# State-space preparation in the bank of the key sums, and five gate tiles tied to products of the last quarter

## The chip, the core and the metric

The kernel runs on one core of one Trainium2 chip. The metric is device time in microseconds (us), as the median of several runs. The core has five engines that run side by side, each working through its own instructions in a fixed order: TensorE (PE in the profile; PEld is its weight load), VectorE (DVE), ScalarE (ACT), GpSimd (POOL) and SyncE (SP, which here issues nearly all DMAs). TensorE writes its results to PSUM, which the kernel uses as eight banks of 512 fp32 values per partition; DVE and ACT read them from there.

## The reference

One layer of a hybrid decoder, for 512 prompt tokens and 64 sampled tokens (8 sequences of 8), 576 tokens together, width 1024:

```python
def layer(h, p, conv_buf, shift_buf, ssm0, wkv0, w):
    mix, ... = token_mixers(rmsnorm(h, w['norm_mix']), conv_buf, shift_buf, ssm0, wkv0, w)
    h = h + mix
    hf = rmsnorm(h, w['norm_ffn'])
    h = h + (jax.nn.silu(hf @ w['w_gate']) * (hf @ w['w_up'])) @ w['w_down']
    gate = jax.nn.sigmoid(rmsnorm(h, w['norm_ple']) @ w['w_ple_gate'])
    h = h + gate * (p.astype(h.dtype) @ w['w_ple_proj'])
    return h, ...
```

`token_mixers` projects the normalised input once (`w_in`) and splits the columns between two groups. Group A is a state-space mixer: a short convolution over x, B and C, then per head a decayed state in chunks of 128 tokens; its output is multiplied by silu(z), where z is one block of eight 128-channel tiles of the projection, and normalised. Group B is a delta-rule mixer (16 heads, 64 x 64 state per head):

```python
s = (s * w_t[:, :, None, :] - s_kk[..., None] * (kk_t * a_t)[:, :, None, :]
     + v_t[..., None] * k_t[:, :, None, :])
return s, jnp.einsum('bhvk,bhk->bhv', s, r_t)
```

Both outputs, side by side, go through `w_out` and are added to h.

## The kernel before

**Layout.** Channels lie on partitions, the 576 tokens on the free axis. A linear product of one 128-channel output tile (`linear`, `mm3`, lines 213 to 215) splits weights and inputs into a high and a low part in fp32r and runs three matmuls for each 128-row block of the weights and each half of the tokens (288). Weights are loaded in blocks of 512 columns (`raw`, three buffers), then split by ACT (`whi`) and by POOL or DVE in turn (`wlo`, line 198), two buffers each.

**Group B.** The heads are taken in four quarters. For each: `prep` (keys, decays), `start_states`, `gram` (small products), `solve` (a triangular inverse, column by column on DVE, lines 654 and 656), `combine` (the two halves of the inverse joined: the products of line 678 and line 692), `chain` (nine windows g of 64 tokens in turn; `core` of a window starts with the products of line 769, then the products of 777, 782, 792, 801) and `head_norm` (the centring products of line 879, token sums, and a norm). `solve` and `combine` of the last quarter are traced after `head_norm` of the third.

**Gate tiles.** The eight z tiles (`zed`: one `linear`, then two ACT passes, one DVE product and a store of `hz` to DRAM) are the last entries of a list of projections. `fill()` takes the next entry. Three z tiles are taken inside `inverse(Q[3])`, between `solve` and `combine`; the other five by the letters "z" of `SEQ = "zzszszszspyw"`, after the last quarter's `chain`. The texts call them z1 to z8.

**State space.** `ssd` is a generator; each "s" of `SEQ` runs it to its next `yield`, and the rest runs after the last head norm. Its preparation: decay rows turned to token order (line 1015), chunk decays (1030), then for five token windows w in the order 1, 2, 3, 4, 0 the B transposes (1044) and the B-C products (1048), and then for each window the x transposes (1065), the scaled x (`xdt`, `xe`) and the state (1078, `hin`). With "p" the per-layer input projection is made, with "y" the finished rows of group B are read back, with "w" one partial output tile. After the generator's end come the output projection (`residual`, line 1265), then `scaled` for the two halves of group A (line 1297).

**PSUM.** Pool `lin` has two tiles of two banks. Pool `sq` has `cx` (two banks), `tr` (one) and `cb` (one). `cb` holds the key sums of `prep` and the start states; it has no other use. When the last head norm is done, `sq` gives way to the pool `ps2`: `r`, `y` (one bank each) and `d` (two).

**Order.** The framework orders each engine's instructions when the program is built: an instruction may run as soon as its inputs, its buffer and its engine are free by the framework's own estimate of durations, and among those that may, the one traced first goes first. The order is then fixed, and semaphores make an engine wait where an input is late. `tc.issue_after(ins)` adds one rule for a block of the program: its instructions on the engine of `ins` are placed behind `ins` in that engine's order. Nothing waits for `ins` to end.

Of the kernel before, what the change touches and what calls it, by code (L numbers as in the profile page):

```python
# [74 lines left out]
def hybrid_step(ctx, tc, A):  # L75
# [20 lines left out]
    def lin_bank():  # L96
        turn[0] += 1
        return lins[turn[0] // 2 % len(lins)].tile([P, 1024], F32, tag="lin", name=nm("lin"))
# [155 lines left out]
    def cb_ps():  # L254
        return bank(sq_, "cb", 1)
# [405 lines left out]
    def combine(s):  # L661

        TT = s.TT = inverses[s.q % 2]
        AA = s2.tile([P, 9, 2, 32], F32, tag="AA", name=nm("AA"))
        for e in range(2):
            for z in range(2):
                r0 = e * 64 + z * 32
                nc.sync.dma_start(TT[r0:r0 + 32, :, :, z * 32:z * 32 + 32].rearrange("s g j t -> s (g j) t"),
                                  s.Td[z, e].rearrange("g s t -> s g t"))
            nc.sync.dma_start(AA[e * 64:e * 64 + 32].rearrange("s g j t -> s (g j) t"),  # L670
                              s.Ad[e].rearrange("g s t -> s g t"))
        Wp = cx_ps()
        Wv = Wp[:].rearrange("p (g j t) -> p g j t", g=8, j=2)
        for g in range(1, 9):
            for jj in jj2:
                for e in range(2):
                    lo_, hi_ = e * 64, e * 64 + 32
                    T.matmul(Wv[hi_:hi_ + 32, g - 1, jj, :], s.Lst[lo_:lo_ + 32, g, jj, 32:64],
                             AA[lo_:lo_ + 32, g, jj, :], start=True, stop=True)
        for e in range(2):  # L680
            hi_ = e * 64 + 32
            if e:
                act(AA[hi_:hi_ + 32, 1:9], Wv[hi_:hi_ + 32], scale=-1.0)
            else:
                V.tensor_scalar(AA[hi_:hi_ + 32, 1:9], Wv[hi_:hi_ + 32], -1.0, None, ALU.mult)
        Xp = cx_ps()
        Xv = Xp[:].rearrange("p (g j t) -> p g j t", g=8, j=2)
        for g in range(1, 9):
            for jj in jj2:
                for e in range(2):  # L690
                    lo_, hi_ = e * 64, e * 64 + 32
                    T.matmul(Xv[lo_:lo_ + 32, g - 1, jj, :], AA[hi_:hi_ + 32, g, jj, :],
                             TT[hi_:hi_ + 32, g, jj, 32:64], start=True, stop=True)
        for e in range(2):
            lo_ = e * 64
            if e:
                act(TT[lo_:lo_ + 32, 1:9, :, 32:64], Xv[lo_:lo_ + 32])
            else:
                V.tensor_copy(TT[lo_:lo_ + 32, 1:9, :, 32:64], Xv[lo_:lo_ + 32])
# [19 lines left out]
    def chain(s):  # L719
# [45 lines left out]
        def core(g):  # L765
            sv = suv(g)
            xw = pairs(cx_ps())
            for jj in jj2:
                T.matmul(xw[:, jj], flat(Gt[:, g, jj, 0]), sv[:, jj, 0], start=True, stop=True)
            xs = sp.tile([P, 2, 64], F32, tag="xs", name=nm("xs"), bufs=2)  # L770
            act(xs[H[0]], xw[H[0], :, 0])
            V.tensor_copy(xs[H[1]], xw[H[1], :, 1])
            ups = cx_ps()
            uw = ups[:].rearrange("p (j v) -> p j v", j=8)
            for jj in jj2:
                for e in range(2):
                    T.matmul(uw[H[e], jj, :], TT[H[e], g, jj, :], xs[H[e], jj, :], start=True, stop=True)
            outs[g] = ow = singles(cx_ps())
            for jj in jj2:
                for e in range(2):  # L780
                    rho = s.Z[H[e], jj, 1, :] if g == 0 else AR[H[e], jj, g]
                    T.matmul(ow[H[e], jj], sv[H[e], jj, 0, e], rho, start=jj == 0, stop=False,
                             skip_group_check=True)
            act(sv[H[0], :, 1, 0], uw[H[0], 0:2, :], scale=-1.0)
            V.tensor_scalar(sv[H[1], :, 1, 1], uw[H[1], 0:2, :], -1.0, None, ALU.mult)
# [62 lines left out]
            if g == 1:  # L848
                sampled()

    YR = []

    def pair(q, name):
        return (se, sp)[q % 2].tile([P, 2, NT], F32, tag=f"bk{q % 2}", name=nm(name), bufs=2)
# [11 lines left out]
    def head_norm(s, ahead=()):  # L866

        q = s.q
        st = tr_ps()[:, 0:20]
        Oc = []  # L870
        gsq = None if ahead else pair(q, "gsq")
        if not ahead:
            ahead = [gate_bonus(2 * q), gate_bonus(2 * q + 1)]
        for jj in jj2:
            o = s.AR[:, jj].rearrange("p g t -> p (g t)")
            sq = gsq[:, jj] if gsq else sp.tile([P, NT], F32, tag="gt", name=nm("gsq"), bufs=2)
            for a, b in HV:
                pp = cx_ps()
                T.matmul(pp[:, 0:HALF], cen[:], o[:, a:b], start=True, stop=True)
                V.tensor_copy(o[:, a:b], pp[:, 0:HALF])  # L880
                act(sq[:, a:b], pp[:, 0:HALF], AF.Square)
            token_sums(st, jj, sq)
            Oc.append(o)
        rn = inv_norm(st, "gnr", 1.0 / 64, GN_EPS)
        for jj in jj2:
            j = 2 * q + jj
            o = Oc[jj]
            gt, y = ahead[jj]
            for a, b, ps in by_channel(rn, jj, cx_ps, "rxg"):
                V.scalar_tensor_tensor(o[:, a:b], o[:, a:b], par("ln_x_w", j), ps, ALU.mult, ALU.mult)  # L890
            (V if q == 3 else G).tensor_tensor(y, y, o, ALU.add)
            yo = sp.tile([P, NT], F32, tag="gt", name=nm("yo"), bufs=2)[:] if q == 2 and jj else y
            V.scalar_tensor_tensor(yo, y, par("ln_x_b", j), gt, ALU.add, ALU.mult)
            if q < 3:
                nc.sync.dma_start(yr_d[j][:], yo)
            else:
                YR.append(split(y, xp, ("xhi", "xlo"), [P, NT], lo_eng=G))

# [39 lines left out]
    def d_ps():  # L938
        return bank(late[2], "d", 2)
# [32 lines left out]
    def ssd():  # L972
# [34 lines left out]
                        ac[:, 64:NT].rearrange("p (b t) -> p b t", b=4), ALU.subtract)  # L1007
        act(de[:], de[:], AF.Exp)
        tk = mt("tk", [P, 5, 3, 16])
        big = lin_bank()  # L1010
        ps = big[:, 0:512]
        for w, (a, m) in enumerate(SW):
            for i, src in enumerate((dt, ac, de)):
                o = (3 * w + i) * 16
# [8 lines left out]
        def sel(h):  # L1023
# [2 lines left out]
        dr = mt("dr", [16, 12, 16])  # L1026
        V.tensor_tensor(dr[:], ident[0:16, 0:16].unsqueeze(1).to_broadcast([16, 12, 16]),
                        al[:].unsqueeze(2).to_broadcast([16, 12, 16]), ALU.mult)
        ps = big[:, 512:1024]
        T.matmul(ps[:, 0:192], ones[0:16, :], dr[:].rearrange("p a b -> p (a b)"), start=True, stop=True)  # L1030
        DEC = mt("DEC", [P, 12, 16])
        act(DEC[:].rearrange("p a b -> p (a b)"), ps[:, 0:192], AF.Exp)
# [5 lines left out]
        xd, hin = {}, [None]  # L1038
        for w in (1, 2, 3, 4, 0):
            a, m = SW[w]  # L1040
            big = lin_bank()
            ps = big[:, 0:512]
            for g in range(2):
                T.transpose(ps[0:m, g * P:g * P + P], BT[g][:, a:a + m], ident[:])
            act(Bt[0:m, w, :], ps[0:m, 0:256])
            ps = big[:, 512:1024]
            for g in range(2):
                T.matmul(ps[0:m, g * m:g * m + m], BT[g][:, a:a + m], CT[g][:, a:a + m], start=True, stop=True)
            if w:
                V.tensor_tensor(CBm[:, :, w - 1, :], ps[:, 0:256].rearrange("p (g q) -> p g q", g=2),  # L1050
                                cmask[:].unsqueeze(1).to_broadcast([P, 2, P]), ALU.mult)
            else:
                V.tensor_tensor(CBd[:], ps[0:64, 0:128].rearrange("p (g q) -> p g q", g=2),
                                dgmask[0:64, 1, :].unsqueeze(1).to_broadcast([64, 2, 64]), ALU.mult)
        yield
        for w in (1, 2, 3, 4, 0):
            a, m = SW[w]
            xt = xd[w] = k4("xdt", [P, D])
            xe = mt("xe", [P, D], bufs=2)
            big = lin_bank()  # L1060
            for h in range(2):
                ps = big[:, h * 512:h * 512 + 512]
                c = slice(h * 512, h * 512 + 512)
                for i in range(4):
                    T.transpose(ps[0:m, i * P:i * P + P], xs[4 * h + i][:, a:a + m], ident[:])
                V.tensor_tensor(h16(xt[0:m, c]), h16(ps[0:m, :]),
                                tk[0:m, w, 0, h * 8:h * 8 + 8].unsqueeze(2).to_broadcast([m, 8, 64]), ALU.mult)
                G.tensor_tensor(h16(xe[0:m, c]), h16(xt[0:m, c]),
                                tk[0:m, w, 2, h * 8:h * 8 + 8].unsqueeze(2).to_broadcast([m, 8, 64]), ALU.mult)
            if w:  # L1070
                if w == 3:
                    yield
                hn = k4("hin", [P, D])
                big = lin_bank()
                for g in range(2):
                    c = slice(g * 512, g * 512 + 512)
                    ps = big[:, c]
                    T.matmul(ps[:], Bt[:, w, g * P:g * P + P], xe[:, c], start=True, stop=True)  # L1078
                    if w > 1:
                        G.tensor_tensor(h16(hn[:, c]), h16(hin[-1][:, c]),  # L1080
# [149 lines left out]
    next(steps)  # L1230
    chain(Q[3])
    parts = 0
    for what in SEQ:
        if what == "z":
            fill()
        elif what == "s":
            next(steps)
        elif what == "p":
# [286 lines left out]
```

## Time and profile before

| | us |
|---|---|
| median of 3 runs | 1372.16 |
| runs | 1371.36 to 1374.79 |
| the profiled execution | 1371.14 |
| its span in the profile | 1369.4 |
| TensorE busy | 1262.0 |
| DVE busy | 718.5 |
| ACT busy | 575.8 |
| POOL busy | 551.2 |

The span is the time between the first and last instruction of the profiled execution. A busy matmul row counts a matmul from its start to its modelled end, and matmuls overlap, so single rows add up to more than the elapsed time; the busy times of a stretch do not. The granted clock is the share of full speed at which TensorE was allowed to run in a stretch. In timeline rows the first number is the start and the second the duration, in us; a bracket at the end gives the idle time before the instruction and what ended it. Most ACT work shows as line 92, a helper, and all linear products as lines 213 to 215; tile names tell them apart.

### The profile page before, as it was taken

To read this page: it belongs to the slowest core of one execution; us is meant where nothing else is said; L and a number is where in the kernel's file an instruction comes from. 1 tells how busy PE (TensorE), PEld (TensorE's weight loads), DVE (VectorE), ACT (ScalarE), POOL (GpSimd) and SP (SyncE) were. 2 spreads that over 40 slices of the span, in tenths; PEclk is the share of its full clock that TensorE was granted. 3 is DMA by queue.
4 is the path that set the end of the run, shared out by engine and by line. 5 is a ranking of instruction groups with operands and counts; after the bars stand their busy time and mean duration, and the time that the engine had idled before them with its cause. 6 is when DMAs were issued, how large, how long until landed. Compare 5 with 4: busy or idle time off the path is not lost.

```text
span 1369.4 us, 26331 instructions
## 1 busy us (share of the span) xinstructions
PE 1262.0 (92%) x10565; PEld 1162.5 (85%) x10565; DVE 718.5 (52%) x1333; ACT 575.8 (42%) x1148; POOL 551.2 (40%) x543
## 2 busy tenths in 40 slices
PE   6897899999989979889969999999999999999996
PEld 5786897889868858777748889999999999999995
DVE  6648767697778787744276674522222221111265
ACT  6565346534662553334433463333233232222253
POOL 5326415632452253124365656433333333343442
PEclk9998999899979989979969999999999999999998
DMA  4322242234223313432625533222322222223332
GB/s 161 123 70 62 84 119 88 70 100 123 67 78 91 104 56 95 131 131 98 191 88 173 185 104 86 67 80 85 80 83 86 83 80 82 81 78 85 125 115 69
DMA packets 94458, 135.56 MB, mean 99 GB/s; under 512 B 34704, under 2 KB 39056, under 8 KB 94336
## 3 DMA queue, kind: packets, MB, share of 16 engines
q1 hardware_dynamic: 94336, 133.88, 32.2%
q8 instruction: 83, 1.36, 0.4%
q14 instruction: 39, 0.32, 0.1%
HBM read 106.10 MB, written 27.75 MB: 98 GB/s over the span
## 4 chain that ended last, share of the span: by engine, by line
PE 41%; DVE 4%; ACT 3%; POOL 2%; DMA 2%; issue 1%; DVEq 0%; ACTq 0%; POOLq 0%
PE lin L215 12%; PE lin L213 12%; PE lin L214 12%; POOL wlo L198 1%; DMA raw<-wts 1%; PE d L1131 1%; PE y L1181 1%; PE d L1143 1%; DVE pg L1373 1%; ACT whi L92 1%; ACT L92 0%; DVE h L1374 0%; ACT wp L92 0%; PE lin L1078 0%; DVE h L1391 0%
## 5 line engine op out<-in xcount | busy, mean ns | idle before, releaser
L213 PE MATMUL lin<-xhi,whi 128*128 128x288 f32 (+1 forms) x1488 | 451.7, 304 | 4.0 <-ACT whi L92 2.2
L215 PE MATMUL lin<-xhi,wlo 128*128 128x288 f32 (+1 forms) x1488 | 448.7, 302 | 2.9 <-POOL wlo L198 2.9
L214 PE MATMUL lin<-xlo,whi 128*128 128x288 f32 (+1 forms) x1488 | 448.8, 302 | 0.0
L198 POOL TENSOR_TENSOR wlo<-raw,whi 128x512 fp32r<-128x512 f32 x136 | 182.1, 1339 | 478.2 <-ACT whi L92 437.1
L92 ACT ACTIVATE whi<-raw 128x512 fp32r<-128x512 f32 (+1 forms) x272 | 168.8, 621 | 408.5 <-PE lin L214 349.2
L213 PEld LDWEIGHTS lin<-xhi,whi 128*128 128x128 f32 (+1 forms) x1488 | 282.3, 190 | 11.3 <-issue 2.8
L215 PEld LDWEIGHTS lin<-xhi,wlo 128*128 128x128 f32 (+1 forms) x1488 | 283.0, 190 | 9.4 <-POOL wlo L198 3.8
L214 PEld LDWEIGHTS lin<-xlo,whi 128*128 128x128 f32 (+1 forms) x1488 | 282.6, 190 | 4.6 <-issue 1.5
L198 DVE TENSOR_TENSOR wlo<-raw,whi 128x512 fp32r<-128x512 f32 (+1 forms) x136 | 95.5, 702 | 165.4 <-ACT whi L92 163.0
L215 PE MATMUL lin<-ah,wlo 128*128 128x288 f32 x352 | 105.1, 299 | 0.9
L213 PE MATMUL lin<-ah,whi 128*128 128x288 f32 x352 | 104.1, 296 | 0.0
L214 PE MATMUL lin<-al,whi 128*128 128x288 f32 x352 | 103.9, 295 | 0.0
L215 PEld LDWEIGHTS lin<-ah,wlo 128*128 128x128 f32 x352 | 66.3, 188 | 3.3 <-POOL wlo L198 2.6
L214 PEld LDWEIGHTS lin<-al,whi 128*128 128x128 f32 x352 | 66.1, 188 | 0.0
L213 PEld LDWEIGHTS lin<-ah,whi 128*128 128x128 f32 x352 | 66.0, 188 | 0.0
L1332 DVE TENSOR_TENSOR sg<-lin,sg 128x576 f32<-128x576 f32 x22 | 16.7, 758 | 82.9 <-PE lin L215 81.7
L1327 DVE TENSOR_TENSOR sg<-lin,rstd 128x576 f32<-128x576 f32 x22 | 16.7, 758 | 69.3 <-PE lin L215 69.0
L654 DVE TENSOR_TENSOR tmp<-L,Tt 72x30 f32<-72x30 f32 (+14 forms) x120 | 50.2, 418 | 3.2
L213 PE MATMUL lin<-xu,whi 128*128 128x288 f32 x128 | 39.8, 312 | 9.1 <-ACT xu L92 7.5
L656 DVE TENSOR_TENSOR Tt<-Tt,tmp 72x30 f32<-72x30 f32 (+14 forms) x120 | 45.1, 376 | 3.5
L215 PE MATMUL lin<-xu,wlo 128*128 128x288 f32 x128 | 39.9, 313 | 6.5 <-DVE wlo L198 5.4
L186 POOL TENSOR_TENSOR al<-sg,ah 128x576 fp32r<-128x576 f32 x22 | 31.5, 1432 | 32.1 <-ACT ah L92 32.1
(364 smaller groups left out, 2516.5 us busy)
## 6 DMA issues: line engine op xcount, KB each, us to landing
raw<-wts SPq DMA_DIRECT2D x271, 256.0 KB, 2.6
S<-s_wkv SPq DMA_DIRECT2D x8, 512.0 KB, 5.0
hd<-s_ssm SPq DMA_DIRECT2D x8, 512.0 KB, 4.8
o_ssm_s<-hd SPq DMA_DIRECT2D x8, 512.0 KB
xbc_d<-E SPq DMA_DIRECT2D x12, 288.0 KB, 2.1
x<-xT SPq DMA_DIRECT2D x8, 288.0 KB
gate_d<-g SPq DMA_DIRECT2D x8, 288.0 KB, 2.6
bv_d<-rw SPq DMA_DIRECT2D x8, 288.0 KB
```

Of the source, the lines that this page charges most:

```text
L92: S.activation(out, in_, func, bias=bias, scale=scale)
L186: eng.tensor_tensor(lo[:], src, hi[:].bitcast(F32), ALU.subtract)
L198: eng.tensor_tensor(lo[:, 0:n], raw[:, 0:n], hi[:, 0:n].bitcast(F32), ALU.subtract)
L213: T.matmul(ps[:, a:b], whi, xhi[:, a:b], start=first, stop=False)
L214: T.matmul(ps[:, a:b], whi, xlo[:, a:b], start=False, stop=False)
L215: T.matmul(ps[:, a:b], wlo, xhi[:, a:b], start=False, stop=last)
L654: V.tensor_tensor(o, L[:, jx:jx + 1, jx + 1:32].to_broadcast([NB, jx, n]), Tt[:, 0:jx, jx:jx + 1].to_broadcast([NB, jx, n]), ALU.mult)
L656: V.tensor_tensor(Tt[:, 0:jx, jx + 1:32], Tt[:, 0:jx, jx + 1:32], o, ALU.subtract)
L1131: T.matmul(yo[(h % 2) * 64:(h % 2) * 64 + 64, (h // 2) * 8:(h // 2) * 8 + 8], hd[:, h * 64:h * 64 + 64], cd[:, h, b * 8:b * 8 + 8], start= ...
L1143: T.matmul(ps[:], bm[:, i, g * P:g * P + P], xst[:, c], start=i == 0, stop=i == 1)
L1327: V.tensor_tensor(s_[:], ps, rs[:], ALU.mult)
L1332: V.tensor_tensor(s_[:], up, s_[:], ALU.mult)
```

## The change

The state-space preparation's tiles move from `lin` to `cb`, with both halves in one bank; the tiles of the later windows (x transposes of w = 4 and 0, states of w = 3 and 4) move to `d`. The kernel records five kinds of small product in `marks` (the last one traced under a key stays), and each of the five z tiles of `SEQ` is placed behind one of them in TensorE's order: z4 behind the last centring product of the third quarter's head norm, z5 behind the last product of line 678 in the last quarter, z6, z7 and z8 behind the first products of windows 1, 2 and 3 of the last quarter's chain.

```diff
-                    T.matmul(Wv[hi_:hi_ + 32, g - 1, jj, :], s.Lst[lo_:lo_ + 32, g, jj, 32:64],
-                             AA[lo_:lo_ + 32, g, jj, :], start=True, stop=True)
+                    marks["c", s.q] = T.matmul(Wv[hi_:hi_ + 32, g - 1, jj, :], s.Lst[lo_:lo_ + 32, g, jj, 32:64],
+                                               AA[lo_:lo_ + 32, g, jj, :], start=True, stop=True)
...
-                T.matmul(xw[:, jj], flat(Gt[:, g, jj, 0]), sv[:, jj, 0], start=True, stop=True)
+                marks[q, g] = T.matmul(xw[:, jj], flat(Gt[:, g, jj, 0]), sv[:, jj, 0], start=True, stop=True)
...
-    YR = []
+    YR, marks = [], {}
...
-                T.matmul(pp[:, 0:HALF], cen[:], o[:, a:b], start=True, stop=True)
+                marks["n", q] = T.matmul(pp[:, 0:HALF], cen[:], o[:, a:b], start=True, stop=True)
...
         tk = mt("tk", [P, 5, 3, 16])
-        big = lin_bank()
-        ps = big[:, 0:512]
+        big = cb_ps()
+        ps = big[:, 0:256]
...
-        ps = big[:, 512:1024]
+        ps = big[:, 256:512]
         T.matmul(ps[:, 0:192], ones[0:16, :], dr[:].rearrange("p a b -> p (a b)"), start=True, stop=True)
...
             a, m = SW[w]
-            big = lin_bank()
-            ps = big[:, 0:512]
+            big = cb_ps()
+            ps = big[:, 0:256]
...
-            ps = big[:, 512:1024]
+            ps = big[:, 256:512]
...
             xe = mt("xe", [P, D], bufs=2)
-            big = lin_bank()
             for h in range(2):
-                ps = big[:, h * 512:h * 512 + 512]
+                ps = cb_ps() if w in (1, 2, 3) else d_ps()
...
                 hn = k4("hin", [P, D])
-                big = lin_bank()
                 for g in range(2):
                     c = slice(g * 512, g * 512 + 512)
-                    ps = big[:, c]
+                    ps = cb_ps() if w < 3 else d_ps()
...
     parts = 0
+    places = [("n", 2), ("c", 3), (3, 1), (3, 2), (3, 3)]
     for what in SEQ:
         if what == "z":
-            fill()
+            with tc.issue_after(marks[places.pop(0)].ins):
+                fill()
```

## The prediction

> **What bounds the kernel now.** I read the page's head, then busy time and granted clock by stretches, then the timeline of each engine where TensorE is not full. TensorE is busy for 92% of the span, so only places where it idles, or runs at half clock, can give time back.
>
> ```profile
> span 1369.4 us, 26331 instructions
> PE 1262.0 (92%) x10565; PEld 1162.5 (85%) x10565; DVE 718.5 (52%) x1333; ACT 575.8 (42%) x1148; POOL 551.2 (40%) x543
> ```
>
> Stretches: start:end, length, then busy time of PE, PEld, DVE, ACT, POOL with counts, granted clock, DMA share, GB/s.
>
> ```profile
> 528.00:569.00 41.00, 40.83 (x357) 37.60 (x357) 36.06 (x92) 14.05 (x31) 6.96 (x8) 1.00 0.37 125
> 569.00:605.00 36.00, 28.04 (x314) 21.64 (x312) 18.33 (x41) 17.13 (x38) 7.68 (x10) 0.67 0.56 171
> 605.00:673.00 68.00, 62.12 (x551) 51.20 (x549) 25.29 (x61) 26.09 (x64) 23.73 (x21) 1.00 0.36 119
> 673.00:686.00 13.00, 13.00 (x86) 10.17 (x86) 2.94 (x6) 6.67 (x13) 8.43 (x6) 0.76 0.54 157
> 686.00:715.00 29.00, 18.66 (x102) 12.34 (x102) 22.71 (x33) 9.44 (x20) 18.07 (x15) 0.62 0.29 103
> 715.00:808.00 93.00, 91.24 (x830) 80.77 (x831) 57.41 (x106) 44.21 (x104) 54.55 (x46) 0.94 0.51 162
> 808.00:839.00 31.00, 30.57 (x267) 29.80 (x266) 19.63 (x25) 11.73 (x19) 20.85 (x14) 1.00 0.24 70
> 900.00:1000.00 100.00, 100.00 (x752) 100.00 (x751) 21.45 (x31) 30.42 (x47) 30.67 (x24) 1.00 0.29 82
> ```
>
> The last row prices a linear matmul: 100/752 = 0.133 us. A gate tile is 8 x 2 x 3 = 48 of them, 6.4 us. Two holes lie in the stage that is changed. From 569 to 605 (end of the third quarter, start of the last quarter's chain) TensorE holds 28.04 x 0.67 = 18.8 us of full-clock work in 36: 17.2 us free. From 686 to 715 it holds 18.66 x 0.62 = 11.6 in 29: 17.4 us free. After 715 it is full (91.24 of 93, 30.57 of 31), so what is put into the holes comes off the end if the state-space part keeps up.
>
> Why gate tiles do not fill the first hole:
>
> ```profile
> 569.76 0.63 ACT L92 ACTIVATE hz<-lin 128x576 f32<-128x576 f32 x1
> 604.83 0.40 PE L1048 MATMUL lin<-bc,bc 128*64 128x64 f32 x4
> 605.15 0.40 PE L213 MATMUL lin<-xhi,whi 128*128 128x288 f32 x1
> 619.27 1.12 PE L1078 MATMUL lin<-xe,Bt 128*128 128x512 f32 x2 [0.51 <-POOL xe L1068]
> 619.83 0.70 PE L213 MATMUL lin<-xhi,whi 128*128 128x288 f32 x1
> ```
>
> The fifth gate tile (z5) is out at 569.76. z6 starts at 605.15, 0.3 us after the last product of the state-space window loop, z7 right after a product of the next step. Both users take `lin` tiles, and these are handed out in the order of the program: z6 stands behind six state-space tiles.
>
> **The change part by part.** No arithmetic is added or removed; buffers move, and five gate tiles get a place in TensorE's order.
>
> A. *z4 and z5 leave the solve stage.* They ran before 569 and may now issue only behind these products, given by line (count: shortest/median/longest ns, first to last start): z4 behind the last L879, z5 behind the last L678, z6 to z8 behind the first three cores of the chain (L769, four matmuls each).
>
> ```profile
> L879 PE MATMUL cx<-ar,cen x4: 406/458/510, 571.6 to 573.1; 128*128 128x288 f32 x4
> 582.31 1.92 PE L678 MATMUL cx<-AA,Lst 32*32 32x32 f32 x64 [0.44 <-DVE ar L890]
> L769 PE MATMUL cx<-suv,G x12: 272/422/582, 588.1 to 612.9; 128*128 128x128 f32 x12
> ```
>
> That takes 12.8 us of TensorE work out of 528 to 569, where DVE sets the pace (36.06 of 41, the solve's row updates, with no TensorE in them). On DVE each gate tile costs one weight half and one product:
>
> ```profile
> 559.10 0.68 DVE L198 TENSOR_TENSOR wlo<-raw,whi 128x512 fp32r<-128x512 f32 x1
> 564.60 0.75 DVE L391 SCALAR_TENSOR_TENSOR hz<-thz,hz 128x576 f32<-128x576 f32 x1
> ```
>
> Best case 2 x 1.43 = 2.9 us gained. Against it: with little left for TensorE its clock may fall, as it did at 569 to 605 (0.67), and the small products then take twice as long (L769: 272 ns at best, 582 at worst). A chain step has four groups of them, together about 1.6 us; the last one and a half steps would lose 2.4 us. I take -1, nearer to the DVE row, because the small products also stop waiting behind gate matmuls. The Trainium skill ("TensorE: Matmul & The Clock Gate", Part 1) says that TensorE drops to half rate after an idle window of about 3.4 us and needs as long a busy one to return. By that rule, with the rows' 2.4 us as its price, this part is +2.4 and the result 1363 instead of 1360; the clock row of 569 to 605 agrees in that a part-filled stretch ran at 0.67, and no run yet shows it for the solve stage.
>
> B. *569 to 605.* z4 and z5 and, from about 589, z6 can run here: 19.2 us into 17.2 us of free time, so about 2 us spill over. The clock stays up: L879, L678, the second product group of the inverse, the chain's first cores. The products on the path at low clock are L678's 1.92 us, the inverse's second group of the same size, the head norm's L879 (four at 0.46) and two L769 groups (four at up to 0.58 each): about 8 us, of which half comes back: -4. Each of some 20 hand-overs now finds one or two gate matmuls in front (0.13 to 0.3 us): +4. Net +2: the -4 and +4 cancel and the spill stays; bounds -2 and +6. The tiles' other work has cover: each brings two weight loads and a store on SP's queue, four ACT passes of 0.63 (2.5 us), one split of 1.27 on POOL, 1.43 on DVE; the stretch holds ACT 17.13, POOL 7.68 and DVE 18.33 of 36. A Tanh between the root and the exponential can add one table load at most:
>
> ```profile
> 569.93 1.27 POOL L198 TENSOR_TENSOR wlo<-raw,whi 128x512 fp32r<-128x512 f32 x1 [7.79 <-ACT whi L92]
> L92 ACT ACT_TABLE_LOAD x2 | 2.6, 1283 | 0.4 <-DVE smask L1004 0.3
> ```
>
> 1.3 us, and not where a Tanh follows an exponential (none is loaded by z6 at 616), so I take nothing.
>
> C. *605 to 673.* Here TensorE is full (62.12 of 68), and one tile (z6) is gone: at the stretch's density of 0.91 that is 6.4 x 0.91 = -5.8, or nothing where the chain's own hand-overs become the bound. z7 and z8 move up inside the stretch; the per-layer projection and the partial output follow them without waiting for state-space tiles, which changes the order and not the sum. A, B and C: -1 + 2 - 5.8 = about -5.
>
> D. *The state-space preparation in one `cb` bank.* Both halves now share a bank and one buffer, so transposes, copy, products and mask of a window follow each other:
>
> ```profile
> L1044 PE MATMUL lin<-ident,bc x2: 474/474/474, 589.4 to 590.0; 128*128 128x128 f32 x2
> L1048 PE MATMUL lin<-bc,bc x20: 219/276/580, 594.9 to 605.0; 128*128 128x128 f32 x16, 128*64 128x64 f32 x4
> 600.04 0.38 ACT L92 ACTIVATE Bt<-lin 128x256 f32<-128x256 f32 x1
> ```
>
> Two transposes at 0.47, the copy 0.38, four products at 0.28 to 0.58, a mask taken as long as the copy: about 3 us a window, 15 us for five, as long as the loop takes now (589.4 to 605.2). The transposes and states of w=1 to 3, ten more fills of the bank, lose the overlap of copy and products, about 1 us each. What needs them is the part after the last head norm, which starts with the rows of L1108 at 692 (below): 0 on the path, covered by the chain from 605 to 673.
>
> E. *686 to 715.* The last windows (w=3 state, w=4, w=0) leave `lin` for the two `d` banks.
>
> ```profile
> L1108 PE MATMUL d<-r,idr x16: 400/401/421, 692.3 to 695.6; 128*128 128x64 f32 x16
> L1078 PE MATMUL lin<-xe,Bt x6: 801/1061/1062, 702.5 to 710.0; 128*128 128x512 f32 x6
> 695.74 1.40 POOL L186 TENSOR_TENSOR xlo<-gb,xhi 128x576 fp32r<-128x576 f32 x1 [1.41 <-ACT xhi L92]
> 714.75 0.61 PE L213 MATMUL lin<-xhi,whi 128*128 128x288 f32 x1
> ```
>
> The output projection's inputs are complete at 695.74 + 1.40 = 697.1, but its first matmul runs at 714.75: until then both `lin` tiles belong to the state-space part. Freed, it can start at about 698. Of these 17 us some 6 are state-space work at full clock, so up to 11 us of projection moves up. Against it: the decay rows (L1108) stood in `d` at 692, beside the `lin` work; now eight tiles take the two `d` banks ahead of them. At about 1 us of products (L1078) and as much of DVE and hand-over, four rounds are 8 to 11 us by which the sampled part starts later. DVE, which is nearly full there (22.71 of 29), would have held part of that anyway. How far it counts is read at the end of the mixing:
>
> ```profile
> L1265 DVE TENSOR_TENSOR h<-lin,yl x1: 757/757/757, 807.9 to 807.9; 128x576 f32<-128x576 f32 x1
> L317 DVE RECIPROCAL rn<-rn x1: 175/175/175, 822.6 to 822.6; 128x5 f32<-128x5 f32 x1
> L1297 DVE TENSOR_TENSOR yl<-lin,bc x1: 757/757/757, 838.7 to 838.7; 128x576 f32<-128x576 f32 x1
> ```
>
> The rows are the last projection tile (L1265), the second root of the state-space part (L317), and the last of the first eight scaled tiles (L1297). The second half of that part is ready at 822.6 and wanted at 838.7: 16 us of slack. So TensorE's gain passes and the delay mostly vanishes in the slack. Bounds -11 and +5; I take -7.
>
> Sum: -5 - 7 = -12. The profiled execution took 1371.14 us (span 1369.4), 1 us under the median of 1372.16; 1371 - 12 = 1359, against the median 1360.
>
> **Rivals.** *Half:* only the first hole pays. In the second, projection matmuls now stand in TensorE's order between the products of a part that starts up to 11 us later; if both together cost it the 16 us of slack and the 7 of E, E is 0: 1372 - 5 = 1367. For it: eight tiles in two banks, and DVE that can't hurry; against it: TensorE, once it has less projection left, is freer for that part. *Nothing:* the work only changes places, since the solve stage idles by what the first hole gains, and the projection's first tile still waits for something else: about 1371. *Slower:* weights behind the state-space loads.
>
> ```profile
> 590.00:595.00 5.00, 3.00 (x32) 2.55 (x31) 2.86 (x9) 3.54 (x7) 0.00 (x0) 0.50 1.00 356
> ```
>
> Just where z5 and z6 shall run, the DMA engines are full with twelve loads of 288 KB, some 10 us at 356 GB/s. TensorE runs in order; a gate tile whose weights lie behind these loads holds the chain's products behind it. One such stall of 11 us, with A at -1 and E halved (-3.5), is +6.5: 1379. It decides from 8 us of stall. For it: the share of 1.00; against it: three raw and two split buffers are loaded ahead.
>
> **How the numbers follow.** Forecast 0.50, half 0.18, nothing 0.14, slower 0.18. Under 0.3% (4 us) a measurement of this kernel can't be told from no change. Faster 0.50 + 0.14 of the half case (which lies just past that bound) = 0.64, same 0.04 + 0.14 = 0.18, slower 0.18. The likeliest case's own range is 1350 to 1367 (E at -11 with C whole and B at -2, or E at -2). Unknown ends widen it: both holes filled whole (about 1346), and the stalled case up to 1377, with a tenth left out above and a little below.
>
> **What would show it.** Gate matmuls between 570 and 605 at a granted clock near 1.0; the last quarter's chain ending about 5 us earlier; the solve stage no longer than 41 us, TensorE part idle in it; the first output projection matmul within 3 us of the last head norm's split; 715 to 839 still full. The prediction is wrong if the chain's first products wait for L213 to L215 or their weights, if the solve stage grows, or if TensorE idles before the second half of the scaled tiles.

## The result, and the profile after

| | before | after |
|---|---|---|
| median, us | 1371.91 (20 runs) | 1365.46 (20 runs) |
| lowest to highest, us | 1368.42 to 1380.77 | 1359.87 to 1371.88 |
| ratio after / before | | 0.9949, 95% interval 0.9932 to 0.9965 |
| the profiled execution, us | 1371.14 | 1370.43 |

The changed kernel is 6.5 us faster (0.51%); forecast were 12. Its profiled execution was one of its slower ones and says by its own total almost nothing, so it is read stage by stage. The page's head, after:

```profile
span 1368.7 us, 26325 instructions
PE 1259.1 (92%) x10565; PEld 1160.4 (85%) x10565; DVE 719.6 (53%) x1333; ACT 577.4 (42%) x1148; POOL 550.2 (40%) x543
```

Five rows of the timelines cut the section that was changed into a front and a back: the first row product of the last solve (L647), the last split of the last head norm (xlo, L186), and the three roots by token of L317 (first and second half of the state-space part, then the feed-forward norm). After:

```profile
537.54 0.69 DVE L647 TENSOR_SCALAR Tt<-L 72x1024 f32<-72x1024 f32 x1 [3.29 <-DMA L<-Ld]
696.40 1.43 POOL L186 TENSOR_TENSOR xlo<-gb,xhi 128x576 fp32r<-128x576 f32 x1 [1.40 <-ACT xhi L92]
807.70 0.19 DVE L317 RECIPROCAL rn<-rn 128x5 f32<-128x5 f32 x1 [1.19 <-ACT rn L92]
829.55 0.19 DVE L317 RECIPROCAL rn<-rn 128x5 f32<-128x5 f32 x1 [0.73 <-ACT rn L92]
881.48 0.19 DVE L317 RECIPROCAL rn<-rn 128x5 f32<-128x5 f32 x1 [2.61 <-ACT rn L92]
```

Before:

```profile
530.26 0.69 DVE L647 TENSOR_SCALAR Tt<-L 72x1024 f32<-72x1024 f32 x1 [3.12 <-DMA L<-Ld]
802.12 0.19 DVE L317 RECIPROCAL rn<-rn 128x5 f32<-128x5 f32 x1 [3.00 <-ACT rn L92]
822.58 0.17 DVE L317 RECIPROCAL rn<-rn 128x5 f32<-128x5 f32 x1
884.12 0.19 DVE L317 RECIPROCAL rn<-rn 128x5 f32<-128x5 f32 x1 [2.61 <-ACT rn L92]
```

Front, from the solve to the split: 165.5 before (the split stood at 695.74), 158.9 after. Back, from the split to the third root: 188.4 and 185.1. All later times are counted from these marks, since the execution after reached the solve 7.3 us late. A second profile of the unchanged kernel (last experiment) was as late, at 537.41, so that lateness needs no change to explain it.

What TensorE did in between, by stretches cut at each kernel's own events: solve, then up to the chain's first product, the chain, the head norm up to the split, and 0 to 20, 20 to 80 and 80 to 120 us behind the split. Columns as in the prediction. Before:

```profile
530.26:566.74 36.48, 36.31 (x307) 33.52 (x306) 33.85 (x89) 13.22 (x28) 6.96 (x8) 1.00 0.33 111
566.74:588.08 21.34, 15.38 (x221) 11.68 (x221) 12.18 (x24) 9.27 (x20) 5.64 (x8) 0.74 0.58 155
588.08:671.30 83.22, 76.84 (x665) 63.16 (x663) 32.53 (x79) 33.49 (x81) 25.77 (x23) 0.92 0.39 132
671.30:695.74 24.44, 19.25 (x122) 15.51 (x118) 12.21 (x21) 9.41 (x17) 11.22 (x8) 0.73 0.63 197
695.74:715.74 20.00, 13.34 (x75) 7.54 (x74) 14.56 (x21) 8.18 (x18) 16.02 (x14) 0.59 0.08 33
715.74:775.74 60.00, 60.00 (x595) 52.72 (x595) 35.62 (x70) 22.27 (x57) 37.27 (x33) 0.96 0.53 174
775.74:815.74 40.00, 38.24 (x300) 34.96 (x300) 29.49 (x46) 25.13 (x51) 22.13 (x15) 0.91 0.42 130
```

After:

```profile
537.54:574.24 36.70, 32.52 (x274) 27.98 (x273) 33.75 (x94) 11.65 (x27) 5.75 (x7) 0.91 0.28 91
574.24:595.82 21.58, 17.84 (x227) 16.50 (x226) 11.06 (x20) 10.22 (x19) 5.62 (x8) 0.76 0.61 170
595.82:674.41 78.59, 77.03 (x694) 63.44 (x689) 32.03 (x79) 34.70 (x85) 26.09 (x24) 1.00 0.44 148
674.41:696.40 21.99, 17.23 (x107) 11.56 (x103) 12.74 (x21) 8.92 (x17) 11.22 (x8) 0.85 0.64 200
696.40:716.40 20.00, 18.85 (x133) 17.35 (x132) 10.74 (x16) 4.40 (x8) 11.28 (x10) 0.99 0.37 117
716.40:776.40 60.00, 60.00 (x625) 53.88 (x625) 39.09 (x70) 26.78 (x65) 40.20 (x35) 1.00 0.47 161
776.40:816.40 40.00, 31.52 (x252) 26.43 (x251) 31.73 (x51) 24.48 (x53) 25.25 (x19) 0.87 0.41 120
```

Take a stretch's length less its busy time times its clock: the TensorE time lost in it (an estimate, as the clock is a mean over the stretch). The first four stretches lose 0.2 + 10.0 + 12.5 + 10.4 = 33.1 us before and 7.1 + 8.0 + 1.6 + 7.3 = 24.0 after. The solve lost more and stayed as long; the chain lost almost nothing and became 4.6 us shorter, the norm 2.4. Behind the split the hole from 0 to 20 is gone (12.1 us lost before, 1.3 after), but a new one stands from 80 to 120 (5.2 before, 12.6 after): 10.8 won and 7.4 given back. From 20 to 80 another 2.4 were lost before and none after, and from 120 to the third root 6.1 and 5.9. In sum the back lost 6.1 us less and became 3.3 shorter, the front 9.1 less and 6.6 shorter: the measure shows where TensorE stood thin, and is good to some 3 us only.

### The profile page after: what moved, and what is told of

It is laid out like the page before. It is cut to its first block, busy times and chain, and to the rows that moved or that the text cites. A ratio compares the mean times of both kernels' runs of the same rounds, so it can differ in the third digit from the quotient of the medians.

```text
span 1368.7 us, 26325 instructions
## 1 busy us (share of the span) xinstructions
PE 1259.1 (92%) x10565; PEld 1160.4 (85%) x10565; DVE 719.6 (53%) x1333; ACT 577.4 (42%) x1148; POOL 550.2 (40%) x543
## 4 chain that ended last, share of the span: by engine, by line
PE 60%; DVE 15%; ACT 5%; DMA 5%; issue 4%; POOL 3%; DVEq 0%; SPq 0%; ACTq 0%; POOLq 0%
PE lin L215 16%; PE lin L213 16%; PE lin L214 16%; DVE h L375 2%; DVE Tt L656 1%; DVE tmp L654 1%; DMA raw<-wts 1%; POOL wlo L198 1%; DVE suv L809 1%; PE cx L777 1%; PE lin L593 1%; PE cx L769 1%; DVE wlo L198 1%; PE cx L792 1%; DVE pg L1373 1%
## 5 line engine op out<-in xcount | busy, mean ns | idle before, releaser
L198 DVE TENSOR_TENSOR wlo<-raw,whi 128x512 fp32r<-128x512 f32 (+1 forms) x136 | 98.4, 724 | 167.4 <-ACT whi L92 164.8
L186 POOL TENSOR_TENSOR al<-sg,ah 128x576 fp32r<-128x576 f32 x22 | 31.5, 1433 | 32.1 <-ACT ah L92 32.1
```

The source lines that it names most:

```text
L186: eng.tensor_tensor(lo[:], src, hi[:].bitcast(F32), ALU.subtract)
L198: eng.tensor_tensor(lo[:, 0:n], raw[:, 0:n], hi[:, 0:n].bitcast(F32), ALU.subtract)
```

## The experiments

Each was timed beside the kernel before on the same chip. Front and back are from one profile each (two of the kernels before and after).

| kernel | ratio to before, 95% interval | front, us | back, us |
|---|---|---|---|
| before, and again | 1; 0.9999 (0.9976 to 1.0023) | 165.5; 164.2 | 188.4; 189.8 |
| after, and again | 0.9949 (0.9932 to 0.9965); 0.9947 (0.9926 to 0.9968) | 158.9; 158.9 | 185.1; 183.3 |
| 1: banks, no ties | 0.9956 (0.9931 to 0.9981) | 163.1 | 188.4 |
| 2: ties alone | 1.0011 (0.9988 to 1.0035) | 164.6 | 186.6 |
| 3: ties, early windows moved | 0.9973 (0.9950 to 0.9997) | 159.6 | 188.8 |
| 4: late windows in r and y | 0.9944 (0.9922 to 0.9966) | 159.8 | 182.6 |
| 5: late windows alone | 1.0002 (0.9977 to 1.0026) | 164.4 | 187.2 |
| 6: early windows alone | 0.9974 (0.9952 to 0.9995) | 159.8 | 189.9 |
| 7: projection held back | 0.9978 (0.9959 to 0.9997) | 159.3 | 191.4 |
| 8: window 0 first | 0.9962 (0.9941 to 0.9984) | 158.0 | 190.1 |
| 9: first half at pair 4 | 0.9959 (0.9943 to 0.9975) | 159.6 | 185.5 |
| 10: first half at pair 3 | 0.9978 (0.9959 to 0.9997) | 159.8 | 182.0 |

**1, no ties; 2, ties alone.** The last lines of the change taken out of the kernel after, and put alone (with `marks`) into the kernel before:

```diff
-            with tc.issue_after(marks[places.pop(0)].ins):
-                fill()
+            fill()
```

> The changed kernel without the five ties: the banks move, the gate tiles z4 to z8 issue where their buffers let them. Theory (the ties pay 5 to 6 us in front of the last chain, the late move to the d banks pays little, because the sampled part starts 12 us later and TensorE idles between 780 and 820 instead of between 686 and 715): 1368 to 1372. Z4 and z5 then run in the solve stage, and 569 to 605 stays thin in TensorE unless z6, no longer behind lin tiles, comes forward by itself. Rival (all of the gain comes from the output projection that starts 26 us earlier, the ties are worth nothing): 1364 to 1367.

> The kernel before with the five ties alone; the state-space preparation keeps its lin tiles. Theory (ties and banks need each other: z4 and z5 leave the solve stage, but z6 still stands behind six lin tiles, and the late hole from 686 to 715 stays): 1367 to 1371, a gain of 0 to 5 us for z4 and z5 in the hole from 569. Rival (the ties are worth nothing): 1371 to 1373. If the ties alone gave the whole 6.5 us, both would be wrong about the banks.

Measured 1366.63 (before: 1372.74) and 1374.31 (a little past the rival's time). The theory fell: it gave the ties 5 to 6 us. By the medians the changed kernel keeps its gain without them (0.9956 against 0.9949), and they alone gain nothing that can be told from none; z6 was out 86.0 us behind the solve's start in run 2, as before. The profile of run 1 says less: its front and back, 351.5 us together, are only 2.4 shorter than before, where the changed kernel's are 10 to 12 shorter.

**3, late windows back in lin; 4, late windows in r and y.**

```diff
-                ps = cb_ps() if w in (1, 2, 3) else d_ps()
+                ps = cb_ps() if w in (1, 2, 3) else (r_ps, y_ps)[h]()
...
-                    ps = cb_ps() if w < 3 else d_ps()
+                    ps = cb_ps() if w < 3 else (r_ps, y_ps)[g]()
```

That is 4; in 3 these tiles are halves of a `lin` tile, as before.

> The changed kernel with the late windows (x transposes of w=4 and w=0, states of w=3 and w=4) back in lin tiles as in the kernel before; the early windows and the ties stay. Theory (the late move gives back what it takes): 1364 to 1367, within 2 us of the changed kernel; the output projection starts at about 715 again, the decay rows at about 690, and TensorE is full from 780 to 820. Rival (the early projection start is the gain): 1370 to 1373.

> The changed kernel with the late windows' eight tiles in the banks r and y, which leaves the d banks to the sampled part. Theory (the d banks' queue delays the decay rows from 692 to 718, and with them the end of the state-space part): the decay rows come back to 690 to 700, the state-space part ends some 8 us earlier, the hole between 780 and 820 shrinks, and the time is 1358 to 1362. Rival (the delay comes from the projection's matmuls, which now stand in TensorE's order between the state-space products, or from VectorE): decay rows stay after 708, and the time is 1364 to 1367.

Run 3: 1369.35, between the two expectations; against the changed kernel the late move would be worth about 3 us, which is not clear of noise (0.0024, each ratio known to 0.002). Run 4: 1365.64, the rival's time, though the theory's mechanism was there: the decay rows came 23 us earlier (1.6 us ahead of the split; 21.7 behind it after), and still the second root came 137.3 us behind the split, against 133.1. When the decay rows run does not decide when the part ends. The first root did come 5.1 us earlier (106.2 against 111.3), and the eighth scaled tile only 1.0 (139.3 against 140.3); the first head pair's first product came no earlier (35.1 against 32.7), probably because the late tiles now stood in the banks `r` and `y`, which the pairs use.

**5, late windows alone; 6, early windows alone.** The kernel before with one half of the bank moves each, no ties.

> The kernel before with the late move alone: the last windows' eight tiles in the d banks; early windows in lin, no ties. The ties measured as worth nothing in both places (with the banks 1.2 us, without them -1.6, each give or take 3). Theory now (the two bank moves add up, about 5 us for the early windows and 4 for the late ones): 1367 to 1370, the output projection starts within 3 us of the last split. Rival (the late move pays only behind the early one): 1371 to 1374.

> The kernel before with the early move alone: the state-space preparation and the windows 1 to 3 in the small bank; late windows in lin, no ties. Theory (the gate tiles come forward by themselves once they no longer stand behind lin tiles, so the early move is worth its 3 to 5 us without ties): 1367 to 1369.5, with all eight gate tiles out by about 600. Rival (tiles that come forward in a bunch leave the chain and the norm thin, so the early move needs the ties): 1371 to 1374.

Run 5: 1374.73 (before 1373.95), a little past the rival's time, with the projection starting as early as expected. Run 6: 1370.02, a gain of 0.26%, a little past the theory's end, and its gate tiles did what the theory said. The ACT rows of the fifth to eighth gate tile there, with no ties:

```profile
571.97 0.63 ACT L92 ACTIVATE hz<-lin 128x576 f32<-128x576 f32 x1
581.17 0.63 ACT L92 ACTIVATE hz<-lin 128x576 f32<-128x576 f32 x1
589.32 0.66 ACT L92 ACTIVATE hz<-lin 128x576 f32<-128x576 f32 x1
596.56 0.63 ACT L92 ACTIVATE hz<-lin 128x576 f32<-128x576 f32 x1
```

All are out 64 us after the solve's start (532.47), where before the eighth came out at 114. The same four stretches of run 6:

```profile
532.47:568.95 36.48, 36.31 (x308) 33.54 (x306) 33.85 (x89) 13.22 (x28) 6.96 (x8) 1.00 0.33 111
568.95:601.30 32.35, 30.20 (x364) 28.76 (x365) 17.98 (x30) 17.75 (x33) 11.21 (x13) 0.99 0.59 180
601.30:672.84 71.54, 65.72 (x562) 50.09 (x561) 29.77 (x75) 30.33 (x76) 28.75 (x26) 0.93 0.49 163
672.84:692.30 19.46, 14.03 (x81) 10.25 (x77) 10.80 (x19) 4.84 (x9) 1.40 (x2) 0.50 0.20 64
```

Here the chain starts 11 us later (the last gate tiles' matmuls stand in TensorE's order in front of its products and of the inverse's, L678) and is 12 us shorter, the norm 5 us. Lost: 0.2 + 2.5 + 10.4 + 12.4 = 25.5 us, against 24.0 with ties and 33.1 before. In these two profiles the ties changed where TensorE stood thin more than how much.

**7, projection held back; 8, window 0 first.** In 7 (with `marks["p", j]` set at the products `y` of head pair j):

```diff
     for c in range(8):
-        ps = lin_ps()
+        with tc.issue_after(marks["p", c - 3].ins) if c > 2 else ExitStack():
+            ps = lin_ps()
...
```

In 8 the loop over the windows runs (1, 2, 3, 0), then come the decay rows and their products, then window 4.

> The changed kernel with the output projection held back: its tiles 3 to 7 each issue only behind the products of one head pair of the state-space part (tile c behind pair c-3), so that this part has TensorE to itself sooner and there is projection left for the hole between 780 and 820. Theory (the projection, standing in TensorE's order between the part's products, is what makes the part end 7 us later): the part ends 5 us or more earlier against the last split than in the changed kernel (133 us), the hole at 780 to 820 closes, and the time is 1359 to 1363. Rival (the part is bound by its own hand-overs between the engines): it ends where it did, the hole moves to about 712 to 725, and the time is 1365 to 1369.

> The changed kernel with the last two windows turned round: window 0, which the sampled part needs, comes before window 4, and the decay rows and their products are put ahead of window 4 in the d banks' queue. Nothing is added. Theory (the late start of the sampled part, 12 us, is what opens the hole between 780 and 820): the decay rows start 4 us or more earlier against the last split than in the changed kernel (21.7 us behind it), the part ends earlier, 1360 to 1364. Rival (the start does not matter, as the r and y banks' run showed, in which the decay rows stood 27 us earlier at the same time): 1364 to 1367.

Run 7: 1370.75, slower than the changed kernel (1365.5 and 1366.2). The part ended later, not sooner (second root 139.4 behind the split), and the hole moved to 20 to 40 us behind the split, as the rival said:

```profile
711.00:731.00 20.00, 13.98 (x119) 11.45 (x118) 10.51 (x21) 9.97 (x22) 10.53 (x9) 0.66 0.12 34
771.00:811.00 40.00, 36.15 (x303) 30.96 (x304) 29.25 (x51) 22.00 (x48) 25.37 (x19) 0.96 0.49 152
```

This does not clear the projection's matmuls, because the run moves them and takes none away. Where DVE takes up a head pair's products (L1182), the first four pairs stood 36, 50, 60 and 70 us behind the split (41, 50, 64 and 73 after), and the last four, among which the held tiles now came, 85, 105, 116 and 131 (84, 98, 111 and 126 after): up to 4.7 us earlier with less of the projection beside them, up to 6.6 later with more.

Run 8: 1368.46, past both expectations. The decay rows started 11.7 us earlier and the first head pair's first product 14 us earlier (18.6 behind the split, 32.7 after); the first pair's products were taken up 8.7 us earlier, the fourth's 3.1 (window 4, which the pairs need too, now came last), and the last pair's came at 123.7 (124.1 after), the first root at 112.2 (111.3) and the second at 134.2 (133.1). So an earlier start of the sampled part (run 4), or of the first pairs as well (run 8), ended the part no sooner. What the projection's matmuls in TensorE's order cost it stays open.

**9 and 10, the gating of the first half moved forward.** One constant, `G0AT = 5` to 4 and to 3.

> The changed kernel as it is, beside its variants on one chip: 1364 to 1367, and a second profile. If the reading by stages holds, the front (start of the solve to the last head norm's split) is 158 to 160.5 us against 165.5 before, and the back (that split to the feed-forward's root) 183 to 187 against 188.4. If the front comes out at 163 or more, the gain of the front was a chance of one profile.

> The changed kernel with the gating of the first half of the state-space part set behind head pair 4 rather than 5 (one constant). Theory (from 80 to 120 us behind the last split TensorE has no projection left and waits for the first root, which the scaled tiles need): the first root comes 5 us or more earlier (111 us behind the split in the changed kernel), the hole shrinks, 1360 to 1364. Rival (VectorE and the hand-overs pace that stretch, so the gating only changes places with the last pairs): the second root comes later by as much (133 now), 1364 to 1368.

> As the run before, with the gating behind head pair 3, the first place where its inputs are complete. Theory: the first root 10 us or more earlier, 1358 to 1363. Rival (VectorE and hand-overs pace the stretch): the first scaled tiles run early, the second half comes 5 to 10 us later, 1365 to 1371.

The changed kernel again: 1366.17 (before 1373.53), front 158.9 and back 183.3, both as expected. Run 9: 1367.44, run 10: 1369.92; the rival's times. The first root came 0.3 us later and 3.4 earlier, not 5 and 10 earlier (111.6 and 107.9 us behind the split, 111.3 after), the second 7 and 13 us later (140.1 and 146.2). Run 10 has the shortest back (182.0), and loses as much behind the third root: 492.5 us to the end, against 487.2 after. What paces the stretch from 80 to 120 shows in the groups by line there, after (busy time and mean ns of one; idle before, and its releaser):

```profile
L1179 PE MATMUL y<-sg,xdt 128*64 128x128 f32 x50 | 4.9, 280 | 3.3 <-POOL sg L1168 3.3
L1153 PE MATMUL r<-r,idr 128*128 128x512 f32 x6 | 2.9, 488 | 1.5 <-ACT er L92 1.5
L1192 DVE TENSOR_TENSOR xs<-xs,hd 128x576 f32<-128x576 f32 x7 | 8.6, 1233 | 1.1 <-DMA hd<-sz_d 0.9
L1202 DVE SCALAR_TENSOR_TENSOR yl<-xs,pv,yh 128x576 fp32r<-128x576 f32 x5 | 7.6, 1531 | 0.5 <-ACT yh L92 0.4
```

TensorE waits in turn for POOL's masked decays, for ACT's exponentials, and behind them DVE is busy 31.73 of 40 us, half of it with the gating (L1192, L1202). No single engine is full there (TensorE 31.52, POOL 25.25, ACT 24.48 of 40); the part goes from hand to hand. That is read from these rows and from runs 7 to 10, which failed to get around it; no run took an engine's share of that work away, so it is not shown.

**The kernel before again.**

> The kernel before, unchanged, for a second profile of it. By stages the changed kernel won 10 to 12 us between the solve and the feed-forward's root in two profiles, and its time fell by only 6.5 to 7.4: 5 to 7 us were lost ahead of the solve, where the order of work is nearly the same, and 1 to 2 behind the root. If these 5 to 7 us are chance, this profile reaches the solve somewhere between 530 and 537, as eleven others did; if they belong to the change, it reaches it at 530 to 531 again. Front 165 to 166, back 187 to 189 either way; the ratio to the kernel before 1 within 0.25 per cent.

Ratio 0.9999, solve reached at 537.41; front 164.2 and back 189.8, each 0.8 us outside what was expected, their sum 354.0 against 353.9. An arrival as late as the changed kernel's comes without the change too.

## Why the prediction was right or wrong

The direction was right and the time lies in the stated range; 12 us were forecast and 6.5 came, nearer to the rival *Half* (1367) than to the forecast (1360). (The ends of the likeliest case, added up from its own terms, are 1352 and 1365, not 1350 and 1367, and no working is given for the 1346.) Seven of the kernels (before, after, runs 1, 2, 3, 5 and 6) give three pairs for each part of the change that differ in that part alone. By the ratios, the ties give +0.11, -0.01 and -0.07%; the early windows -0.26% alone, -0.38% behind the ties, -0.46% beside the late ones; the late windows +0.02% alone, -0.18% and -0.24% behind the early ones. Each difference is known to some 0.3%, a mean of three to some 0.2% (estimated from the intervals). So the early windows are worth 0.37%, 5 us, which is clear of noise; the late ones 0.13%, 2 us, which is not; the ties 0.01%.

The lengths of the stretch from the solve to the third root don't agree on the ties. It took 353.9 us before and 351.2 in run 2, 349.8 in run 6 and 348.5 in run 3, 351.5 in run 1 and 343.9 and 342.3 after: in all three pairs the kernel with the ties is shorter, by 1.3 to 9.2 us. With 351.5 us, and 486.0 behind them, run 1's median execution would have had to reach the solve at 527 us, earlier than any of the 14 profiles (529.8), so its one profile may not be typical. What the ties are worth is open.

**A, solve stage (-1).** It took 36.7 instead of 36.5. The two gate tiles did leave it, and TensorE's idling there cost nothing; the 1 us forecast as won didn't come either. By the rule that the Trainium skill states ("TensorE: Matmul & The Clock Gate", Part 1), the prediction's rival put this part at +2.4. The trace agrees that the clock falls in a part-filled stretch, though the longest single idle time there was 2.85 us, less than the window of the rule: the clock was 0.91 in the stage and 0.68 at its end.

```profile
564.00:574.00 10.00, 9.14 (x73) 6.79 (x73) 8.70 (x29) 2.05 (x6) 1.08 (x2) 0.68 0.11 39
```

But the solve waits for DVE's rows, and the third quarter's chain (its last state step on DVE, L809) ran 6.5 us ahead of the solve's end, where before it ran 1.7 us behind it. So the clock fell and the price didn't come.

**B, the hole behind the solve (+2).** +0.2 (21.34 to 21.58), from a gain and a loss that cancel. The products of L678 came 2.3 us earlier behind the solve's end (13.3 instead of 15.6), probably because the third quarter was done sooner. From them to the chain's first product it took 8.3 us instead of 5.8. Before (L678 started at 582.31, in the prediction) and after:

```profile
586.24 1.91 PE L692 MATMUL cx<-TT,AA 32*32 32x32 f32 x62 [0.31 <-ACT AA L92]
588.08 1.22 PE L769 MATMUL cx<-suv,G 128*128 128x128 f32 x4
```

```profile
587.51 1.92 PE L678 MATMUL cx<-AA,Lst 32*32 32x32 f32 x64
589.36 0.61 PE L213 MATMUL lin<-xhi,whi 128*128 128x288 f32 x1
590.20 0.59 ACT L92 ACTIVATE AA<-cx 32x512 f32<-32x512 f32 x1 [1.95 <-DVE AA L685]
594.69 1.20 PE L692 MATMUL cx<-TT,AA 32*32 32x32 f32 x64
595.82 0.71 PE L769 MATMUL cx<-suv,G 128*128 128x128 f32 x4
```

After, the inputs of L692 are complete at 590.79, but 22 gate matmuls (589.36 to 594.69), z5 behind its tie, stand in front of it in TensorE's order: 3.9 us of waiting. So about the 4 us put down for hand-overs did come, in one place rather than over 20, and nearly as the sign of being wrong that the prediction named, one step ahead of the chain's first products. The 4 us to be won by the clock came in small part: the stretch ran at 0.76 (0.74 before), not near 1.0, and L678 took 1.92 us as before; L692 fell from 1.91 to 1.20. That the sum came out near is luck.

**C, chain (-5.8).** The chain was 4.6 shorter, and the head norm, which I had not counted, 2.4. A, B and C: -5 forecast, -4.2 by the first profiles; the whole front with the norm, -6.6 by the first profiles and -5.3 by the second. So the size of the sum was nearly right, partly because terms that were off cancelled (A and B) or were made up by the norm. "z6 stands behind six state-space tiles" is borne out: with the ties alone z6 came out as late as before (run 2), and taking those tiles out of `lin` lets z6 to z8 come forward by themselves (run 6). That A and B, which were put down to the ties, won anything is not shown.

**D, small bank.** The window loop took 24.5 us, not 15, and its last mask moved from 75.1 to 95.5 us behind the solve's start. Its first reader runs behind the split (L1116, at 723.01), so nothing waits for it: 0, as forecast.

**E, late windows (-7).** By the ratios this is the term that was sized wrong. The projection did start at the split (0.4 us ahead of it, 19.0 behind it before), and its last tile was done at 81.4 us behind the split instead of 112.1. The marks that the prediction took, and the first scaled tile, after:

```profile
777.75 0.76 DVE L1265 TENSOR_TENSOR h<-lin,yl 128x576 f32<-128x576 f32 x1
809.95 1.42 DVE L1297 TENSOR_TENSOR yl<-lin,bc 128x576 f32<-128x576 f32 x2 [0.91 <-ACT bc L92]
836.67 0.76 DVE L1297 TENSOR_TENSOR yl<-lin,bc 128x576 f32<-128x576 f32 x1 [2.41 <-PE lin L215]
```

The eighth scaled tile (836.67) stands 140.3 us behind the split, 143.0 before: 2.7 won, not 7 (4.1 by the second profiles, 144.2 to 140.1). The sampled part's first products came 13.8 us later against the split (16.1 to 29.9), not 8 to 11, and the slack for them was read off one root where there are two. The second one still had room (829.55 against 836.67). The first one, which lets the first scaled tiles leave `lin`, had 12.7 us before (802.12 against 814.84); after, DVE stands waiting for ACT's copy of it, and two finished tiles then leave `lin` at once (the row with x2). It came 4.9 us later (106.4 to 111.3 behind the split), and the projection, which before had filled TensorE up to then, was out 30 us ahead of it. TensorE idled before the second half of the scaled tiles, the sign that the prediction named for itself as wrong. That the first root is what holds E back is argued from these rows; run 4, where it came 5.1 us earlier, won 1.0 at the eighth scaled tile. E is worth 2 us by the ratios, give or take 2 to 3, and 3.3 and 6.5 by the backs of the two pairs of profiles.

Of the rivals, *Half* described E's fate and gave 1367; its reason (projection matmuls between the part's products) is neither shown nor refuted by run 7. *Slower* did not come: where the loads lie after, some 6 us later than before, the DMA share is full again and TensorE was never without work.

```profile
595.00:600.00 5.00, 5.00 (x88) 4.78 (x81) 4.10 (x10) 2.85 (x6) 0.00 (x0) 1.00 1.00 353
600.00:605.00 5.00, 5.00 (x54) 4.66 (x52) 1.42 (x4) 1.88 (x4) 1.27 (x1) 1.00 1.03 393
```

What stays open: from the solve to the third root the changed kernel is 9.9 and 11.6 us shorter, and 1 to 2 us longer from there to the end (485.3 and 485.6 before, 487.2 and 486.5 after), which is more than the 6.5 to 7.4 us of the medians. The ten profiles of kernels with the early windows moved reached the solve at 534.4 us in the mean, the four without at 532.3; among arrivals from 529.8 to 537.5 that doesn't say whether the other 2 us are chance. So it stays open whether the 5.5 us that are missing from the forecast lie in E, as the ratios have it, or in good part outside the stretch that the prediction added up.

## What to carry to other kernels

When work is moved up to fill a hole, look at the place it came from: TensorE's filler is a fixed stock, and here a hole came back where the stock ran out, because what stood there did not end sooner as well. Read the slack at each of a delayed part's results, the first of them too, and not at its last alone. A tile tied behind one product can stand in front of the next one on the path, as z5 did for 3.9 us. And where tiles of two parts are handed out from one pool in program order, parting the pools can do what an order written out by hand is meant to do; try the one without the other before keeping both.

## What the runs showed that was not expected

The same program reaches the same place at very different times. Two profiles of the unchanged kernel came to the solve at 530.26 and 537.41, and then took 353.9 and 354.0 us to the third root. The second execution was 3.6 us behind at 450 us and 7.2 behind at the solve, so half of the difference arises in a stretch of small products, at another clock; first profile, then second:

```profile
456.00:530.00 74.00, 61.81 (x723) 48.96 (x722) 50.70 (x101) 40.48 (x94) 32.44 (x36) 0.91 0.29 83
```

```profile
456.00:530.00 74.00, 61.60 (x697) 49.53 (x697) 51.11 (x103) 39.67 (x91) 29.24 (x34) 0.86 0.26 74
```

For these two kernels, the length of a stretch between two events repeated better than a profile's total: to 0.1 us before and 1.7 after, where the totals differ by 7.5 and 4.5. No other kernel was profiled twice, and the profile of run 1 warns against reading more out of a single one.
